# Two layer-norm joints, a residual put off and a pooling mixer rewritten as matrix products in a 256-token transformer kernel

## The chip, the cores and the metric

The kernel runs on one core of a Trainium2 chip, whose engines are TensorE (PE, with its weight loads PEld), VectorE (DVE), ScalarE (ACT), GpSimd (POOL) and SyncE (SP, which issues most DMAs). The metric is the device time of one launch in microseconds (us). The kernel before took 1624.29, 1628.38 and 1629.59 us in three runs, median 1628.38.

## The reference, cut to what matters

The model has two blocks over 256 tokens of width 1024, all in fp32. The first block has a hybrid mixer and a feed-forward, each closed by a layer norm (the two joints of this case). The second block has two layers of feed-forward, mixer, cross attention and feed-forward; the mixer of its first layer is the pooling mixer.

```
mod = silu(c) @ w_ada + b_ada ; sh1, sc1, g1, sh2, sc2, g2 = split(mod, 6)
y = hybrid_mixer(x*(1+sc1) + sh1)
x = layer_norm(ALPHA*x + (1+g1)*y, ln1_g, ln1_b)          # joint 1
h = x*(1+sc2) + sh2
ff = square(relu(h @ w_ff_in)) @ w_ff_out
x = layer_norm(ALPHA*x + (1+g2)*ff, ln2_g, ln2_b)         # joint 2
for i in 0, 1:
    x = x + 0.5*swiglu_ffn(rms_norm(x, ffn1_norm[i]), ...)
    h = rms_norm(x, mix_norm[i])
    # i = 0: four groups of 256 channels, windows 2, 4, 8, 16
    #   p = trailing causal mean of h over the window, minus h
    #   x = x + (p @ pool_w[group] + pool_b)*pool_scale
    # i = 1: native sparse attention
    x = x + memory_cross_attention(rms_norm(x, xattn_norm[i]), mem, ...)
    x = x + 0.5*swiglu_ffn(rms_norm(x, ffn2_norm[i]), ...)
return rms_norm(x, final_norm)
```

## The kernel before, in words

**Products.** An fp32 operand is kept as a pair of fp32r tiles, `hi` (rounded) and `lo` (the rest). `mm3` issues three products per pair: hi by hi, hi by lo, lo by hi. The 256 tokens are two tiles of 128. Activations that feed products are the pairs `hTh`, `hTl` (8 chunks of 128 features by 256 tokens) or `A0`, `A1` (hidden units).

**Weights.** Class `Weights` brings every weight in portions of 1 MB by SP's DMA into one of four buffers `w`. Each is split in quarters, `hi` by a cast on ACT (L183) and `lo` by a subtraction on DVE (L184), into one of three pairs, or into a further pair on activation buffers that are free just then (`W.pairs`, `into=`). The split runs two portions ahead of its use. One portion feeds 48 products of 256 columns. A list written out at the start fixes the order of the portions; at some of them (table `ADA`) it adds a step of the conditioning vector `mod`: no product, but two DVE instructions over 128x1024 (L581).

**Order.** The program text gives each engine one in-order queue. The framework works with priorities in program order; `tc.high_priority()` puts what is inside ahead of other ready work of the engine, and `tc.issue_after` holds an instruction behind another.

**Output projections.** `out_proj` (L435) accumulates both token tiles in PSUM and holds back the last 8 k. It does these for tile 0, calls `cb(0)` (residual, norm), does them for tile 1 (48 products of 512 columns: 8 k, 2 halves, 3 products), calling `tr(0)` (transposes of tile 0 for the next product) after the sixth k, and then calls `cb(1)`. The final projection of the kernel instead goes half by half (`halves=True`).

**The next input phase.** `in_phase` (L469) does its first three portions by token tiles: it issues `tr1` (transposes of tile 1), does tile 0 for three portions (72 products of 256 columns), then tile 1, and from the fourth portion on it goes feature-major over both tiles. So three portions of work on tile 0 stand over tile 1's norm.

**Joint 1** (L937 to L963). `layer_norm_stats`: per half of 512, DVE multiplies the product by the gate row (L942), adds ALPHA*x (L943) into a buffer `rr` of its own and takes BN_STATS (L944); then BN_AGGR (L946), the epsilon (L948), and the power on POOL (L949). `cb_ln1` normalises on DVE (L957, two instructions) and lets POOL make the residual x = r*ln1_g + ln1_b (L959, L960). `tr_ln1` transposes r on PE (L401), applies gain and shift four chunks each on DVE (L422, tile `m`) and ACT (L420), and splits `m` into `hTh` (ACT, L393) and `hTl` (DVE, L394).

**Joint 2** (L1080 to L1103). `cb_ln2` norms on DVE with the ln2 rows (L1084, L1085); `tr_ln2` transposes, and `gained` multiplies by the next norm's gain on DVE (L408), casts on ACT (L393) and subtracts on DVE or POOL (L394).

**Norm** (L1028 to L1076) serves the rms norms of block 2. `feed(q)` takes a quarter of x (2 chunks), writes x*gain as `hTh` (ACT, L1044) and `hTl` (DVE, L1045), squares it on ACT (L1050) and adds the squares into `sq` (L1051; POOL for quarters 1 and 2, DVE for 3). `sums`, `cols` and `r` give 1/rms as a column per token or a row over the partitions; consumers multiply by it after their products.

**Pooling mixer** (L1287 to L1339). It forms the row r, h = x*r, log2(window) shifted additions per quarter with ACT copying the first columns (L1308), divides and subtracts h (L1307 to L1314), splits (L1317), multiplies by `pool_w` (48 products of 256 columns on the `acc` banks), and adds to x. Three of the four value portions of the cross attention's memory (`kv_proj`, 48 products each, evacuated by ACT at L1324) stand over the pooling work, the fourth stands behind it; the mixing norm's gain enters at the split.

Of the kernel before, what the change touches and what calls it, by code (L numbers as in the profile page):

```python
# [198 lines left out]
def tile_model(ctx: ExitStack, tc: tile.TileContext, I, out):  # L199
# [71 lines left out]
    for i, k in enumerate([("win", j) for j in range(11, 22)] + [("wout", 0)] + [("ffi", j) for j in range(1, 5)]):  # L271
        ADA[k] = 8 + i
# [162 lines left out]
    def out_proj(act, nk, key, cb, tr, k0=0, ks=None, accs=None, last=8, mid=5, halves=False):  # L435
# [25 lines left out]
        cb(1, accs[1])  # L461
# [469 lines left out]
    ln1g, ln1b = load_rows("s8_0", "ln1_g", "ln1_b")  # L931
    rr = sb("s8_3", [P, 2, D])
# [4 lines left out]
    def layer_norm_stats(t, a, row, x):  # L937
        r = rr[:, t]
# [722 lines left out]
```

## Time and profile before

| | |
|---|---|
| runs | 1624.29, 1628.38, 1629.59 us |
| profiled execution | 1626.63 us, span 1624.9 us, mean granted PE clock 0.993 |
| PE busy | 1582.5 us (97%) |
| DVE, ACT, POOL busy | 1063.9 (65%), 836.6 (51%), 261.5 (16%) us |
| joint 1, 289 to 326 us | PE busy 31.56 of 37.00, granted clock 0.91 |
| joint 2, 484 to 523 us | PE busy 36.11 of 39.00, granted clock 1.00 |
| pooling stage, 692 to 729 us | PE busy 33.36 of 37.00, granted clock 0.95 |

Since PE is busy 97% of the span, the places to read are those where it is not, and those where its granted clock falls. Other engines' idle time matters only where PE waits for them. A clock column of 0.50 is the lower of two levels (1.2 against 2.4 GHz).

### The profile page before, as it was taken

The page shows a single profiled execution, that of the slowest core. Times are in us where ns is not written, and L with a number is a line of the kernel's source. Part 1 is how long each engine was busy: PE and PEld are TensorE (multiplying, and loading weights), DVE is VectorE, ACT ScalarE, POOL GpSimd, SP SyncE. Part 2 cuts the span into 40 slices and gives each one's busy share as a digit, 9 for nine tenths or more (in the row PEclk, how much of TensorE's full clock was granted, in tenths as well). Part 3 has the DMA queues.
Part 4 walks back from the last instruction along what each step waited for, and adds up shares of the span by engine and source line. Part 5 has one row for each costly group of instructions (what it writes and reads, how often), then busy time and mean ns, then how long its engine had stood idle before and what let it go on. Part 6 is the DMA issues. An engine that isn't in the chain of part 4 may idle for free.

```text
span 1624.9 us, 29581 instructions
## 1 busy us (share of the span) xinstructions
PE 1582.5 (97%) x12110; PEld 1514.5 (93%) x12110; DVE 1063.9 (65%) x1938; ACT 836.6 (51%) x1720; POOL 261.5 (16%) x266
## 2 busy tenths in 40 slices
PE   7999999899999999999999999999999999999998
PEld 7999998798988999989999999999989999999897
DVE  8889977874548655586665457544678566575453
ACT  4565446364535544465554445443546675464442
POOL 2003002320301110130121012201200211022011
PEclk9999999999999999999999999999999999999999
DMA  8874766475545555524365545544445223365530
GB/s 321 335 290 154 295 249 221 151 278 203 182 156 208 208 182 208 182 104 182 130 227 188 183 156 208 182 182 156 178 171 207 79 104 131 130 222 185 197 136 27
DMA packets 43432, 304.21 MB, mean 187 GB/s; under 512 B 5008, under 2 KB 5264, under 8 KB 7328
## 3 DMA queue, kind: packets, MB, share of 16 engines
q1 hardware_dynamic: 39312, 283.66, 48.3%
q0 software_dynamic: 2112, 10.49, 1.8%
q10 hardware_dynamic: 1872, 8.17, 1.3%
q8 instruction: 95, 1.56, 0.4%
q14 instruction: 41, 0.34, 0.1%
HBM read 294.96 MB, written 7.34 MB: 186 GB/s over the span
## 4 chain that ended last, share of the span: by engine, by line
PE 62%; DVE 4%; ACT 2%; issue 1%; POOL 0%; POOLq 0%; DVEq 0%; ACTq 0%
PE wk L232 21%; PE ck L232 20%; PE acc L232 19%; DVE lo L184 1%; ACT hi L183 1%; DVE s L1411 0%; DVE m L1307 0%; PE ck L1537 0%; DVE hTl L1045 0%; PE ck L1538 0%; PE ck L1539 0%; ACT s L183 0%; DVE m L408 0%; PE ck L1265 0%; DVE hTl L394 0%
## 5 line engine op out<-in xcount | busy, mean ns | idle before, releaser
L183 ACT CAST hi<-w 128x512 fp32r<-128x512 f32 (+1 forms) x708 | 417.0, 644 | 406.5 <-issue 251.2
L184 DVE TENSOR_TENSOR lo<-w,hi 128x512 fp32r<-128x512 f32 (+1 forms) x708 | 496.8, 745 | 147.8 <-ACT hi L183 144.1
L232 PE MATMUL wk<-hTl,hi 128*128 128x256 f32 x992 | 281.3, 284 | 1.5 <-DVE hTl L1045 1.5
L232 PE MATMUL wk<-hTh,hi 128*128 128x256 f32 x992 | 282.5, 285 | 0.0
L232 PE MATMUL wk<-hTh,lo 128*128 128x256 f32 x992 | 281.1, 283 | 0.0
L394 POOL TENSOR_TENSOR A<-m,A 128x256 fp32r<-128x256 f32 x119 | 135.7, 1146 | 666.3 <-ACT A L393 653.2
L183 ACT CAST s<-w 128x512 fp32r<-128x512 f32 x224 | 126.1, 617 | 138.5 <-issue 85.3
L232 PEld LDWEIGHTS wk<-hTl,hi 128*128 128x128 f32 x992 | 187.5, 189 | 2.7 <-DVE hTl L1045 1.9
L232 PEld LDWEIGHTS wk<-hTh,hi 128*128 128x128 f32 x992 | 187.5, 189 | 0.9 <-issue 0.2
L232 PEld LDWEIGHTS wk<-hTh,lo 128*128 128x128 f32 x992 | 187.2, 189 | 0.1
L232 PE MATMUL acc<-A,hi 128*128 128x256 f32 x1024 | 185.2, 283 | 0.9 <-ACT A L393 0.9
L184 DVE TENSOR_TENSOR s<-w,s 128x512 fp32r<-128x512 f32 x224 | 146.3, 697 | 53.5 <-ACT s L183 51.6
L232 PEld LDWEIGHTS acc<-A,hi 128*128 128x128 f32 x1024 | 157.0, 189 | 1.4 <-ACT A L393 1.1
L232 PE MATMUL ck<-hTh,hi 128*128 128x256 f32 x528 | 149.1, 282 | 0.0
L232 PE MATMUL ck<-hTh,lo 128*128 128x256 f32 x528 | 148.7, 282 | 0.0
L232 PE MATMUL ck<-hTl,hi 128*128 128x256 f32 x528 | 148.7, 282 | 0.0
L232 PE MATMUL acc<-A,lo 128*128 128x256 f32 x512 | 143.3, 280 | 0.0
L232 PE MATMUL acc<-hi,A 128*128 128x512 f32 x432 | 139.9, 398 | 0.0
L232 PE MATMUL ck<-hTh,s 128*128 128x256 f32 x672 | 123.7, 282 | 0.0
L232 PEld LDWEIGHTS ck<-hTh,s 128*128 128x128 f32 x672 | 105.5, 190 | 0.0
L232 PEld LDWEIGHTS ck<-hTh,hi 128*128 128x128 f32 x528 | 99.5, 188 | 0.1
L232 PEld LDWEIGHTS ck<-hTl,hi 128*128 128x128 f32 x528 | 99.4, 188 | 0.1
(407 smaller groups left out, 3162.7 us busy)
## 6 DMA issues: line engine op xcount, KB each, us to landing
w<-in_ffn_i SPq DMA_DIRECT2D x88, 1024.0 KB, 4.8
w<-in_ffn_o SPq DMA_DIRECT2D x44, 1024.0 KB, 4.8
w<-in_ada SPq DMA_DIRECT2D x24, 1024.0 KB, 5.5
w<-in_win SPq DMA_DIRECT2D x22, 1024.0 KB, 7.1
w<-in_xkv SPq DMA_DIRECT2D x16, 1024.0 KB, 6.2
w<-in_ffi SPq DMA_DIRECT2D x16, 1024.0 KB, 4.8
w<-in_ffo SPq DMA_DIRECT2D x16, 1024.0 KB, 4.8
w<-in_nin SPq DMA_DIRECT2D x10, 1024.0 KB, 4.8
```

The source lines that it names most:

```text
L183: nc.scalar.copy(h[:, sl], t[:, sl])
L184: nc.vector.tensor_tensor(lo[:, sl], t[:, sl], h[:, sl].bitcast(F32), op=OP.subtract)
L232: T.matmul(o, lhsT=lhsT, rhs=rhs, start=start, stop=stop)
L394: i = (lo or V).tensor_tensor(dst[1], src, dst[0].bitcast(F32), op=OP.subtract)
```

## The change

It has six parts.

1. **Joint 1 and the residual.** The residual sum is written into x itself, with a scratch tile for the product; `rr` is gone. The normalisation is done by ACT (Identity, scale rs, bias -mu*rs, the bias by one small DVE instruction). The multiplication and addition of ln1_g and ln1_b (`x_ln1`, POOL) are put off: they are issued after the input phase of the first group of the feed-forward, with the loads of their rows into the buffers `s8_3` and `s8_0`, where ln2's rows follow.
2. **Weights.** The first input portion `ffi 0` is split into the pair `s8_3`, `s8_0`, free now; four steps of the conditioning vector move from `ffi` 1 to 4 to `ffo` 0, 2, 4, 6; one release of pairs goes.
3. **Projections.** In `out_proj` `cb` and `tr` have high priority, and tile 1's held products are taken as four k with both halves, then four k for half 0, then four k for half 1; the final projection loses its own order. In `in_phase` tile 1's transposes have high priority, and the splits of portions 1 and 2 are no longer held behind a cast.
4. **Joint 2.** `tr_ln2` makes `hTh` (ACT) and `hTl` (DVE) straight from the transposes in PSUM, eight instructions each of 128x128.
5. **Norm.** All additions into `sq` go to DVE.
6. **Pooling mixer.** The norm before it now splits x*gain. PE multiplies that by `pool_w` first (48 products of 256 columns), ACT scales by 1/rms per token, and PE multiplies by a constant matrix (`poolm`, the window means less the identity, in fp32), both token tiles; DVE adds to x. The two halves of the quarters stand between the memory's value portions.

```diff
 with_ada("wout", 4, 8)
-    with_ada("ffi", 0, 8)
-    add("ffo", 0, 8)
+    add("ffi", 0, 1, into=("s8_3", "s8_0"))
+    with_ada("ffi", 1, 8)
+    with_ada("ffo", 0, 8)
...
-        cb(0, accs[0])
-        for hs in ((0,), (1,)) if halves else ((0, 1),):
-            for n, k in enumerate(range(end - hold, end)):
-                go(k, 1, hs)
-                if n == mid and not halves:
+        with tc.high_priority():
+            cb(0, accs[0])
+        half = end - hold // 2
+        order = [(k, (0, 1)) for k in range(end - hold, half)] + [(k, (h,)) for h in range(2) for k in range(half, end)]
+        for n, (k, hs) in enumerate(order):
+            go(k, 1, hs)
+            if n == mid:
+                with tc.high_priority():
                     tr(0)
...
-            V.tensor_tensor(r[:, sl], a[:, h], row[:, sl], op=OP.mult)
-            V.scalar_tensor_tensor(r[:, sl], x[:, sl], ALPHA, r[:, sl], op0=OP.mult, op1=OP.add)
-            V.bn_stats(st[:, h], r[:, sl])
+            r = m3([P, 512])
+            V.tensor_tensor(r, a[:, h], row[:, sl], op=OP.mult)
+            V.scalar_tensor_tensor(x[:, sl], x[:, sl], ALPHA, r, op0=OP.mult, op1=OP.add)
+            V.bn_stats(st[:, h], x[:, sl])
...
+        off = stat()
+        V.scalar_tensor_tensor(off, mu, -1.0, rs, op0=OP.mult, op1=OP.mult)
-            V.tensor_scalar(r[:, sl], r[:, sl], mu, rs, op0=OP.subtract, op1=OP.mult)
+            A.activation(r[:, sl], r[:, sl], AF.Identity, scale=rs, bias=off)
-        G.tensor_tensor(xs[t], r, ln1g, op=OP.mult)
-        G.tensor_tensor(xs[t], xs[t], ln1b, op=OP.add)
...
+    def x_ln1():
+        ln1g, ln1b = load_rows("s8_3", "ln1_g", "ln1_b")
+        for t in range(2):
+            G.tensor_tensor(xs[t], xs[t], ln1g, op=OP.mult)
+            G.tensor_tensor(xs[t], xs[t], ln1b, op=OP.add)
+        ln2.extend(load_rows("s8_0", "ln2_g", "ln2_b"))
...
-                (V if q == 3 else G).tensor_tensor(self.sq, self.sq, t, op=OP.add)
+                V.tensor_tensor(self.sq, self.sq, t, op=OP.add)
...
-        gained(ps, t, n1.pr, n1.g)
+        for k in range(8):
+            p, g = ps[:, k // 4, k % 4], n1.g[:, k:k + 1]
+            last["hi"] = A.activation(n1.pr[0][:, k, TS[t]], p, AF.Copy, scale=g)
+            V.scalar_tensor_tensor(n1.pr[1][:, k, TS[t]], p, g, n1.pr[0][:, k, TS[t]].bitcast(F32), op0=OP.mult, op1=OP.subtract)
...
+        ps = bank(q, (P, 2, 256))
+        for t in range(2):
+            for k in range(2):
+                mm3(ps[:, t], pick(pg, ALL, 2 * q + k, TS[t]), pick(wpool, ALL, 2 * q + k), start=k == 0, stop=k == 1)
+        us.append(ps)
...
+    def pooled(q):
+        u = m3([P, 2, 256])
+        for t in range(2):
+            A.activation(u[:, t], us[q][:, t], AF.Copy, scale=rc[:, t:t + 1])
+        ps = ck((P, 2, S))
+        for f in range(2):
+            c = slice(f * P, f * P + P)
+            mm(ps[:, f], u[:, 0, c], mixed[0][:, q, 0:S], stop=False)
+            mm(ps[:, f, P:S], u[:, 1, c], mixed[0][:, q, S:S + P], start=False)
...
+    kv_proj(0, v_keep, 4, 5)
+    pooled(0)
+    pooled(1)
+    kv_proj(0, v_keep, 5, 6)
+    pooled(2)
+    pooled(3)
+    kv_proj(0, v_keep, 6, 8)
```

How the order changes is shown at three places. On PE at joint 1, `s_3_252` (before) and `x_236` (after) are what is transposed for tile 0; the `acc<-hi,A` rows are tile 1's held products. Before, 38 of the 48 stand ahead of the transposes:

```order
L232 MATMUL acc_2938<-lo_3119,A_235_2873 128x512
L232 MATMUL acc_2938<-hi_3118,A_235_2873 128x512
L232 MATMUL acc_2937<-s_158_3142,A_235_2873 128x512
L232 MATMUL acc_2937<-s_258_3143,A_235_2873 128x512
L401 MATMUL acc_3255<-ident,s_3_252_2934 128x128 x4
L401 MATMUL acc_3256<-ident,s_3_252_2934 128x128 x4
L232 MATMUL acc_2937<-s_158_3142,A_235_2873 128x512
L232 MATMUL acc_2938<-s_158_3142,A_235_2873 128x512
```

In the changed kernel 23 stand ahead of them:

```order
L241 MATMUL acc_2932<-hi_3060,A_235_2871 128x512
L241 MATMUL acc_2932<-lo_3061,A_235_2871 128x512
L407 MATMUL acc_3245<-ident,x_236_2872 128x128 x4
L241 MATMUL acc_2932<-hi_3060,A_235_2871 128x512
L407 MATMUL acc_3246<-ident,x_236_2872 128x128 x4
L241 MATMUL acc_2931<-hi_3112,A_235_2871 128x512
L241 MATMUL acc_2931<-lo_3113,A_235_2871 128x512
```

So the transposes of tile 0 moved forward by 15 products: 25 products stand behind the first four of them (24 behind the rest) instead of 10. On DVE at the same place, from tile 0's statistics to its gain and shift, before (`w_3417` is a step of the conditioning vector, `lo` the splits of weights):

```order
L944 BN_STATS bnst_3200<-s_3_252_2934 128x6 x2
L581 SCALAR_TENSOR_TENSOR w_3417,modc<-w_3417,xn_117 128x1024
L184 TENSOR_TENSOR lo_3167<-w_3164,hi_3166 128x512 x4
L946 BN_AGGR stat_3207<-bnst_3200 128x2
L184 TENSOR_TENSOR lo_3342<-w_3339,hi_3341 128x512
L948 TENSOR_SCALAR stat_3209<-stat_3207 128x1
L184 TENSOR_TENSOR lo_3342<-w_3339,hi_3341 128x512
L957 TENSOR_SCALAR s_3_252_2934<-s_3_252_2934,stat_3207,stat_3210 128x512 x2
```

and in the changed kernel (L963 makes the bias for ACT's normalisation):

```order
L951 BN_STATS bnst_3194<-x_236_2872 128x6 x2
L953 BN_AGGR stat_3203<-bnst_3194 128x2
L955 TENSOR_SCALAR stat_3205<-stat_3203 128x1
L193 TENSOR_TENSOR lo_3337<-w_3334,hi_3336 128x512
L963 SCALAR_TENSOR_TENSOR stat_3209<-stat_3203,stat_3206 128x1
L193 TENSOR_TENSOR lo_3337<-w_3334,hi_3336 128x512 x2
L428 TENSOR_SCALAR m_268_3255<-acc_3245,gn_3106 128x128 x4
```

The step of the conditioning vector and four splits no longer stand between BN_STATS and BN_AGGR, and L957 has left DVE. On ACT in the pooling stage, before, with the evacuation of a memory portion (L1324) among the copies of first columns:

```order
L1308 COPY m_432_7408<-s_2_424_7381 128x2
L1324 COPY s_4_442_7459<-wk_7472 128x2x256
L1308 COPY m_434_7422<-s_2_424_7381 128x2
L1317 ACTIVATE hTh_7382<-m_430_7394,vecs 128x256 x2
L1317 ACTIVATE hTh_7382<-m_432_7408,vecs 128x256 x2
L1308 COPY m_435_7425<-m_434_7422 128x2x2
L183 CAST hi_7524<-w_7522 128x512 x4
```

and in the changed kernel (L1337 scales a quarter's product by 1/rms, here those of quarters 2 and 3; L1058 and L1064 are the feed of the next norm):

```order
L1064 ACTIVATE m_440_7557<-x_357_5171 128x512
L1337 ACTIVATE m_442_7622<-acc_7422,rcol_7455 128x256 x2
L1332 COPY s_4_431_7458<-wk_7572 128x2x256
L192 CAST hi_7662<-w_7660 128x512 x4
L1058 ACTIVATE hTh_7533<-x_358_5172,vecs 128x256 x2
L1064 ACTIVATE m_444_7638<-x_358_5172 128x512
L1337 ACTIVATE m_445_7641<-acc_7440,rcol_7455 128x256 x2
```

The scaling of the last quarter (`m_445`) has come to stand behind an evacuation, four casts of weights and one feed.

## Rows read from the trace of the kernel before

**Rows 1.** Page, part 1: busy time, share of the span, instructions.

```profile
PE 1582.5 (97%) x12110; PEld 1514.5 (93%) x12110; DVE 1063.9 (65%) x1938; ACT 836.6 (51%) x1720; POOL 261.5 (16%) x266
```

**Rows 2.** Waits of PE: what waits, its releaser, us in all, times, longest.

```profile
PE wk L232 <- DVE hTl L394: 3.9, 2, 1.9
...
PE acc L232 <- ACT hTh L1317: 2.6, 1, 2.6
...
PE wk L232 <- DVE hTl L1045: 1.5, 2, 0.9
...
PE acc L401 <- DVE s L1085: 1.1, 1, 1.1
PE ck L994 <- DVE m L1197: 1.1, 1, 1.1
```

**Rows 3.** Windows: stretch, us, busy per engine (instructions), PE clock, DMA share, GB/s.

```profile
289.00:326.00 37.00, 31.56 (x184) 28.09 (x184) 33.39 (x56) 14.20 (x29) 13.95 (x8) 0.91 0.44 156
484.00:523.00 39.00, 36.11 (x242) 32.29 (x242) 34.81 (x69) 22.28 (x52) 7.72 (x10) 1.00 0.50 184
692.00:729.00 37.00, 33.36 (x260) 32.51 (x259) 32.83 (x58) 24.31 (x59) 13.85 (x11) 0.95 0.33 114
307.10:310.50 3.40, 3.40 (x18) 3.40 (x17) 3.40 (x8) 0.00 (x0) 0.00 (x0) 0.50 0.02 5
```

**Rows 4.** Chain that ended last: start, us, engine, output, line, instructions.

```profile
538.27 5.70 PE wk L232 x48
```

**Rows 5.** Timeline of PE, joint 1: start, us, engine, line, operation, [idle before <-releaser].

```profile
299.82 2.54 PE L232 MATMUL acc<-s,A 128*128 128x512 f32 x10
...
305.59 0.38 PE L232 MATMUL wk<-hi,hTl 128*128 128x256 f32 x1 [1.94 <-DVE hTl L394]
...
317.05 0.39 PE L232 MATMUL wk<-hi,hTh 128*128 128x256 f32 x1 [0.86 <-ACT hTh L393]
319.94 0.39 PE L232 MATMUL wk<-hi,hTl 128*128 128x256 f32 x1 [1.92 <-DVE hTl L394]
```

**Rows 6.** Timeline of DVE, joint 1.

```profile
289.26 1.37 DVE L942 TENSOR_TENSOR s<-acc,s 128x512 f32<-128x512 f32 x2 [2.96 <-PE acc L232]
290.55 1.28 DVE L943 SCALAR_TENSOR_TENSOR s<-x,s 128x512 f32<-128x512 f32 x2
291.75 1.28 DVE L944 BATCH_NORM_STATS2 bnst<-s 128x6 f32<-128x512 f32 x2
...
294.08 2.49 DVE L184 TENSOR_TENSOR lo<-w,hi 128x512 fp32r<-128x512 f32 x4
296.49 0.20 DVE L946 BATCH_NORM_AGGREGATE stat<-bnst 128x2 f32<-128x12 f32 x1
...
301.15 1.62 DVE L184 TENSOR_TENSOR lo<-w,hi 128x512 fp32r<-128x512 f32 x1
...
303.29 2.85 DVE L394 TENSOR_TENSOR hTl<-m,hTh 128x512 fp32r<-128x512 f32 x2
```

**Rows 7.** Timeline of POOL, joint 1.

```profile
297.39 0.93 POOL L949 TENSOR_TENSOR stat<-stat,mhalf 128x1 f32<-128x1 f32 x1 [24.26 <-DVE stat L948]
299.43 2.78 POOL L959 TENSOR_TENSOR x<-s,s 128x1024 f32<-128x1024 f32 x1 [1.12 <-DVE s L957]
```

**Rows 8.** Timeline of ACT, joint 1 and the pooling stage.

```profile
300.16 1.51 ACT L420 ACTIVATE m<-acc,gn 128x128 f32<-128x128 f32 x4 [2.59 <-PE acc L401]
301.55 1.15 ACT L393 CAST hTh<-m 128x512 fp32r<-128x512 f32 x2
...
719.10 2.18 ACT L183 CAST hi<-w 128x512 fp32r<-128x512 f32 x4
```

**Rows 9.** Groups by form, 742 to 800 us: instructions, then busy us, mean ns, idle before.

```profile
L232 PE MATMUL ck<-m,s 128*128 128x256 f32 x32 | 7.6, 379 | 0.0
```

**Rows 10.** Timeline of DVE, a feed at 1362 us.

```profile
1362.39 1.92 DVE L1045 SCALAR_TENSOR_TENSOR hTl<-x,vecs,hTh 128x256 fp32r<-128x256 f32 x2
```

**Rows 11.** Timeline of POOL at the same feed.

```profile
1362.36 1.28 POOL L1051 TENSOR_TENSOR sq<-sq,m 128x512 f32<-128x512 f32 x1 [1.65 <-ACT m L1050]
```

More of the change, by code (lines that the diff above doesn't have):

```diff
@@ L62, in pack_half, with pool_mix @@
     return np.concatenate([pack_rows(w[:512]), pack_cols(w[512:], 512)])
+def pool_mix():
+    t = np.arange(S)
+    blocks = []
+    for win in POOL_WINDOWS:
+        back = t[None] - t[:, None]
+        m = ((back >= 0) & (back < win)) / np.minimum(t + 1, win)[None] - (back == 0)
+        blocks.append(np.concatenate([m[:P], m[P:, P:]], axis=1))
+    return np.ascontiguousarray(np.concatenate(blocks, axis=1).astype(np.float32))
 def lay_out(i):
@@ L270, in tile_model @@
     ADA = {}
-    for i, k in enumerate([("win", j) for j in range(11, 22)] + [("wout", 0)] + [("ffi", j) for j in range(1, 5)]):
+    for i, k in enumerate([("win", j) for j in range(11, 22)] + [("wout", 0)] + [("ffo", j) for j in range(0, 8, 2)]):
         ADA[k] = 8 + i
@@ L433, in tile_model, with out_proj @@
     ALL = slice(None)
-    def out_proj(act, nk, key, cb, tr, k0=0, ks=None, accs=None, last=8, mid=5, halves=False):
+    def out_proj(act, nk, key, cb, tr, k0=0, ks=None, accs=None, last=8, mid=5):
         ks = nk if ks is None else ks
@@ L471, in in_phase @@
         pss, pending = [], []
-        hi0 = last["hi"]
         if first:
-            tr1()
+            with tc.high_priority():
+                tr1()
         for i in range(first):
             pss.append(ring(i, (P, 2, 256)))
-            with tc.issue_after(hi0.ins) if i else ExitStack():
-                w = W.get(keys[i])
-            tok_proj(w, hT(), 0, pss[i][:, 0])
+            tok_proj(W.get(keys[i]), hT(), 0, pss[i][:, 0])
         for i, key in enumerate(keys):
@@ L983, in ffw @@
             in_phase(keys_in[k0 // per:(k0 + g) // per], hT, tr_in, *evac_of(hid), first if n == 0 else 0)
-            if n and between:
-                between()
+            between(n)
             accs = out_proj(lambda k: hid(k - k0), nk, key_out, next_cb, next_tr, k0, g, accs, **kw)
@@ L1105, in tile_model @@
     ffw([("ffi", j) for j in range(16)], "ffo", hT2, lambda: tr_ln1(1), ev_relu2, 2, 32, (16, 16), cb_ln2, tr_ln2,
-        between=lambda: row_of(g2p, modc[:, 40:48]))
+        between=lambda n: row_of(g2p, modc[:, 40:48]) if n else x_ln1())
     def ft_lead(parts, k0, nk=8, begin=True, between=None):
@@ L1290, in tile_model, with pool_load @@
     V.tensor_tensor(psb, vec("pool_b"), vec("pool_scale"), op=OP.mult)
-    ffn("ffn1", 0, n1, add_x_from(npool, n1, 0.5, False), lambda: mem_load(0))
-    npool.sums()
-    r = npool.r()
-    hp = sb("s8_2", [P, 8, S])
-    pT = pair_tile(("hTh", "hTl"))
-    ng = vec("mix_norm0")
-    nx = Norm("xattn_norm0")
-    for q in (3, 0, 2, 1):
-        E = V if q > 1 else G
-        sl = slice(2 * q, 2 * q + 2)
-        h = hp[:, sl]
-        E.tensor_tensor(h, xq(q), rows2(r), op=OP.mult)
-        src = h
-        for lv in range(q + 1):
-            d = 1 << lv
-            dst = m3([P, 2, S])
-            E.tensor_tensor(dst[:, :, d:], src[:, :, d:], src[:, :, :S - d], op=OP.add)
-            A.copy(dst[:, :, 0:d], src[:, :, 0:d])
-            src = dst
-        win = POOL_WINDOWS[q]
-        ed = m3([P, 2, 16])
-        E.tensor_tensor(ed, src[:, :, 0:16], pinv[:, q].unsqueeze(1).broadcast_to([P, 2, 16]), op=OP.mult)
-        V.scalar_tensor_tensor(src[:, :, 16:], src[:, :, 16:], 1.0 / win, h[:, :, 16:], op0=OP.mult, op1=OP.subtract)
-        E.tensor_tensor(src[:, :, 0:16], ed, h[:, :, 0:16], op=OP.subtract)
-        for f in range(2):
-            k = 2 * q + f
-            A.activation(pT[0][:, k], src[:, f], AF.Copy, scale=ng[:, k:k + 1])
-            V.scalar_tensor_tensor(pT[1][:, k], src[:, f], ng[:, k:k + 1], pT[0][:, k].bitcast(F32), op0=OP.mult, op1=OP.subtract)
-            x = xq(q)[:, f]
-            A.activation(x, x, AF.Identity, bias=psb[:, k:k + 1])
+    wpool, mixed = [], []
+    def pool_load():
+        mem_load(0)
+        mixed.append(sb("s8_2", [P, 4, 384]))
+        G.dma_start(mixed[0].rearrange("p q t -> p (q t)"), I["poolm"])
+    ffn("ffn1", 0, n1, add_x_from(npool, n1, 0.5), pool_load)
+    wpool = W.get(("pw", 0))
+    pg = npool.hT()
+    us = []
+    for q in range(4):
+        ps = bank(q, (P, 2, 256))
[3 more added lines that the diff above has]
+        us.append(ps)
+        if q == 2:
+            npool.sums()
+    rc = npool.cols()
+    nx = Norm("xattn_norm0")
     KV[0] = kv_tiles()
@@ L1642, in tile_model @@
             x_tok()
-        accs = out_proj(lambda k: hid(k - k0), NKF, "ffn2o1", cb_final, lambda t: None, k0, g, accs, halves=True)
+        accs = out_proj(lambda k: hid(k - k0), NKF, "ffn2o1", cb_final, lambda t: None, k0, g, accs)
         k0 += g
```

35 lines of the change are left out of this document (11 added, 24 removed).

## The prediction

> **What bounds the kernel now.** I read the busy times first: PE is busy 1582.5 of 1624.9 us [rows 1], so about 42 us of the span are its idle time, and no edit that only relieves another engine counts unless it shortens a wait of PE, makes its products fewer, or keeps its clock up. Second, the waits of PE [rows 2]: among the longest are waits for hTl of joint 1 (3.9 us in two), for hTh of the pooling mixer (2.6 in one), for hTl of the feeds (1.5 in two), and 1.1 us twice at joint 2. All of them lie where the change works. Third, the windows on the three stages [rows 3]: joint 1 leaves PE idle for 37.00 - 31.56 = 5.4 us, joint 2 for 2.9, the pooling stage for 3.6. The clock column adds something: 0.91 in joint 1 and 0.95 in the pooling stage. In one stretch of 3.40 us right behind a wait the granted clock was 0.50, that is the 1.2 GHz level, with PE busy all of it on about 16 to 18 products [rows 3]; 48 such products take 5.70 us at 2.4 GHz, 0.119 each [rows 4], so those 16 or so were worth 1.9 us and 1.5 were lost. Joint 1's 0.91 over 37 us is 3.3 us, two such stretches (one behind each of the 1.9 us waits [rows 5]), the pooling stage's 0.05 x 37 = 1.9 about one. So joint 1 loses 5.4 + 3.0 = 8.4 us, the pooling stage 3.6 + 1.5 = 5.1, joint 2 2.9.
>
> **Joint 1, tile 0.** Before, BN_STATS ends at 291.75 + 1.28 = 293.0 and BN_AGGR starts at 296.5, since a step of the conditioning vector and four subtractions (2.49) stand between [rows 6]. In the new order nothing stands there, so x is normed some 3.4 us earlier: BN_AGGR and the epsilon until 293.4, POOL's power 0.93 [rows 7] until 294.3, the small bias until 294.5, and two ACT instructions over 512 columns, which I put at a cast's 2.18 / 4 = 0.55 each [rows 8], give the halves at 295.1 and 295.6. PE starts tile 1's products when DVE is released, at 289.3 [rows 6]; one takes 0.24 (ten from 299.82 in 2.54, the end of the last included [rows 5]). The transposes stand behind 23 of them: 23 x 0.24 = 5.5, at 294.8. They now wait 0.3 to 0.8 at their new place; I take 0.35, as the first four need one half only. Behind them come 25 products, 6.0 us, instead of 10, 2.4. What has to fit under these is gain and shift (1.51), casts (1.15) [rows 8] and hTl. Before, hTl's two instructions took 2.85 and one subtraction 1.62, beside POOL's residual [rows 6, 7]; four subtractions without it took 2.49, 0.62 each [rows 6], so the two hTl would take some 1.25. In all 1.5 + 1.2 + 1.25 = 3.9 of the 6.0: the 1.94 us wait goes, and the half-clock stretch behind it.
>
> **Joint 1, tile 1.** From the end of its last product: half 1's three DVE passes 0.65 each, 1.95 (half 0 has had 12 products, 2.9 us, for its own); 0.34 for aggregate and epsilon, 0.93 for the power, 0.1, 1.1 for the normalisation, 0.9 for eight transposes of 128 columns (half of the 0.2375 that 256 columns of fp32 take [rows 9]), 1.5 for gain and shift, 0.6 for the first cast: 7.4 to hTh, about 8.7 to the last hTl. The cover is tile 0's 72 products, 72 x 0.119 = 8.6. It just fits, with weight splits between it on DVE and ACT; I take waits of 0.75 together, with the ends at 0 and at the 0.86 + 1.92 of before [rows 5]. No half clock is then to be expected, since it came behind waits of 1.9. Joint 1 loses 0.35 + 0.75 = 1.1: a gain of 7.3. Ends: 8.4 when nothing waits, 3.75 when tile 1's 2.8 stay, with 0.35 and one half-clock stretch of 1.5.
>
> **The put-off residual.** POOL's two passes per tile (2.78 each [rows 7]) move from the joint into the first input phase, four of them, 11 us, some 20 to 25 us after the joint. There they run beside DVE's subtractions for weights. In the rows DVE's lo took 1.62 instead of 0.62 and the two hTl 2.85 instead of 1.25: 2.6 us lost to two POOL passes [rows 6], so 5.2 to four. A weight portion is 5.7 us of products [rows 4] and two are split ahead, 11.4 of cover, and the conditioning steps left this stretch. I take 0; without this cover it costs 5.2.
> The Trainium skill's "SBUF — State Buffer", "Who interferes with whom", speaks against this edit: a DVE instruction with two SBUF inputs contends with a GpSimd instruction that reads SBUF, and the lock is exclusive. The row 1.62 against 0.62 agrees that they contend, though not for a whole pass; by the rule DVE would stand for all 11 us, which is the rival C below, still inside 11.4 of cover if that is there.
> Splitting the first portion into the freed pair only lets it be ready earlier: 0.
>
> **Joint 2.** It keeps its DVE norm passes. Tile 0's transposes also move ahead, which costs a wait of about 0.5, and its new eight short instructions on each of ACT and DVE replace three dependent steps. For tile 1 the half order gives the 1.14 us wait back in part only, because high priority also moves these transposes ahead; I leave 1.2 there and 0.7 for splits of weights that are late. The 1.09 us wait behind it [rows 2] should go, as DVE has fewer passes there. 2.9 - 2.4 = 0.5 gained. Between -1.5 (the norm's DVE chain now waits at both places) and 2.5.
>
> **Pooling stage.** Both kernels have 192 products for the memory's values and 48 by pool_w, 240 x 0.119 = 28.6 us. The window of 37.00 us [rows 3] holds 260 instructions of PE, 240 of them these; some 0.6 of it belongs to the neighbours, so 36.4, and 7.8 for the rest: 5.1 lost, 2.7 for sums and row. After, the mixing matrix adds per quarter two fp32 products of 256 columns and two of 128. The trace has 32 instructions of fp32 by 256 columns in 7.6 us [rows 9], 0.2375 each; such a product is a pair of them, 0.475, the narrow one about 0.24: 4 x 2 x 0.715 = 5.7. Sums stay, about 1.0. The new wait is for ACT: the last quarter's scaling stands behind an evacuation (0.5), four casts (2.18 [rows 8]) and a feed (three passes like these casts, some 1.5), with its own two passes of 0.4 that is 5.0, under 27 products, 3.2. That bounds it by 0 and 1.8; I take 0.6, since most of what stands ahead of it can run before its quarter's turn. 5.7 + 1.0 + 0.6 = 7.3: a gain of 0.5. Between -2 (the full 1.8 and a touch of half clock) and 1.05. The stage trades waits for products, almost even.
>
> **Feeds.** Without POOL's addition of 1.28 [rows 11] beside it, two hTl take less than 1.92 [rows 10]; by the ratio above about 0.9. DVE takes over an addition of some 0.65 each. Of 1.5 us waits [rows 2] I take 1.0 back; between -0.5 (the addition stands ahead of hTl) and 1.5. The final projection: half 0's last pass has 12 products, 2.9 us, over it and needs some 1.5, so 0.
>
> **Sum.** 7.3 + 0.5 + 0.5 + 1.0 = 9.3 us. From the profiled execution's 1626.6 that is 1617.3, from the median 1628.4 it is 1619.1 (the profiled one lies 1.8 below the median). I forecast 1618.2. All lower ends together give a gain of -0.25, all upper ends 13.5.
>
> **Rivals.**
> A, no wait left: the joints stop waiting at all. For it: x is earlier than the old place by far. Against: the new places are earlier too. Gain 13.5: 1627.5 - 13.5 = 1614.0, from halfway between the two bases.
> B, waits only move: the transposes wait at their new place as long as at the old, and hTl of tile 1 still comes 2.8 late with PE's clock halved behind. For it: DVE is busy 33.39 of 37.00 us in joint 1 [rows 3], so what leaves it is filled by weight splits that were behind; high priority puts products behind a transpose that isn't ready. Against: the order shows the splits gone from between the statistics. Joint 1 gains 8.4 - 2.8 - 3.0 - 0.35 = 2.25, the rest nothing: 1625.3.
> C, slower: in the first input phase DVE's two-input instructions stand still for as long as POOL's four passes run, 4 x 2.78 = 11.1 us, and the splits are not two portions ahead, because DVE came out of joint 1 with no slack. Then PE waits for lo the whole 11.1 us and loses two half-clock stretches, 3.0: 1627.5 - 7.3 + 11.1 + 3.0 = 1634.3. It decides once the splits lead by less than one portion (5.7 us) when POOL starts. For it: DVE's 90% in joint 1, and 1.62 against 0.62. Against: DVE lost half of POOL's time there, not all, and the steps of the conditioning vector have left.
>
> **How the numbers follow.** Forecast 0.62 (own range 1613 to 1623), A 0.12, B 0.18, C 0.08. About 0.3%, 4.9 us, is what a measurement of this kernel can tell from no change, so faster is below 1623.5: the forecast's cases and A, 0.74; within it B, 0.18; slower C, 0.08. The range reaches to B and to A's side: 1611 to 1626, leaving out C and some of each edge.
>
> **What would show it.** Right: the transposes of tile 0 at about 295 with a wait under 0.8; PE's idle time in joint 1 near 1 us and a granted clock of 1.00 there; no POOL pass of 2.7 us beside the splits before 315; the fp32 products of the mixer near 0.475; no wait above 1 us in the pooling stage; hTl of the feeds at 0.45 each. Wrong: a new PE wait for lo within 30 us behind joint 1 (C), a clock still below 0.95 in joint 1 (B), a pooling stage of more than 38 us (ACT's queue), or a gain that sits in none of these stages.

## The result and the profile after

The changed kernel took 1615.03 us (median of four runs, 1614.0 to 1617.07) against 1627.55 for the kernel before in the same comparisons: ratio 0.9925, 95% interval 0.9912 to 0.9937. Forecast were 1618.2 and a range of 1611 to 1626. Its profiled execution has a span of 1613.7 us. The page's first part, which answers to [rows 1]:

```profile
PE 1579.8 (98%) x12138; PEld 1513.7 (94%) x12138; DVE 1053.2 (65%) x1937; ACT 841.7 (52%) x1729; POOL 220.3 (14%) x239
```

The same views as in [rows 2, 3] show that the long waits of the three stages are gone. Waits of PE (waiting tile, releaser, us in all, times, longest):

```profile
PE acc L407 <- DVE x L1099: 1.1, 1, 1.1
PE acc L407 <- ACT x L966: 0.9, 2, 0.5
...
PE wk L241 <- DVE hTl L1059: 0.5, 1, 0.5
...
PE wk L241 <- ACT hTh L399: 0.2, 1, 0.2
```

Windows (stretch, us, busy and instructions of PE, PEld, DVE, ACT, POOL, PE clock, DMA share, GB/s), for joint 1, joint 2 and the pooling stage:

```profile
289.00:326.00 37.00, 35.86 (x247) 32.69 (x246) 28.50 (x57) 22.48 (x46) 4.17 (x7) 1.00 0.50 164
477.00:516.00 39.00, 37.57 (x258) 34.00 (x257) 36.49 (x77) 26.19 (x64) 4.19 (x5) 1.00 0.51 186
683.20:718.80 35.60, 35.60 (x286) 34.91 (x285) 21.54 (x42) 20.94 (x44) 0.73 (x1) 1.00 0.36 122
```

Joint 1 leaves 1.14 us idle instead of 5.44 at a clock of 1.00 instead of 0.91, joint 2 1.43 instead of 2.89, the pooling stage nothing instead of 3.64, at 1.00 instead of 0.95. PE's timeline has three waits left in joint 1, where [rows 5] had the two of 1.9 us:

```profile
297.18 0.66 PE L407 MATMUL acc<-ident,x 128*128 128x128 f32 x4 [0.46 <-ACT x L966]
...
310.84 0.66 PE L407 MATMUL acc<-ident,x 128*128 128x128 f32 x4 [0.46 <-ACT x L966]
314.30 0.51 PE L241 MATMUL wk<-s,hTh 128*128 128x256 f32 x2 [0.22 <-ACT hTh L399]
```

To see where the time came from I cut PE's timeline at the same six products in every kernel: the transposes of the mixer's output ahead of joint 1 (263.35 before, 264.97 after), the first product of the feed-forward's output projection (359.25, 352.73), the second product of its second group (451.79, 444.87), the first product of ffn1's output projection (583.80, 574.91) and of its second group (669.58, 660.69), and the first scores of the cross attention behind the pooling mixer (752.52, 742.34). Differences give the stretches in us; "joint 1" is the first, "pooling" the last. The stretch between the two groups of ffn1 is 85.78 in every kernel. The first three expectations measure joint 1 up to an earlier product (73.0 before, 64.9 after); the difference is the same 8.1.

| kernel | joint 1 | first group | joint 2 | pooling | total, median |
|---|---|---|---|---|---|
| before | 95.90 | 92.54 | 132.01 | 82.95 | 1627.55 |
| after | 87.76 | 92.14 | 130.04 | 81.65 | 1615.03 |
| plain first portion (one run) | 97.31 | 92.55 | 131.52 | 81.67 | 1625.35 |
| residual at once | 97.86 | 92.14 | 130.25 | 81.79 | 1624.17 |
| before, no residual | 88.84 | 92.14 | 132.47 | 83.07 | 1620.84 |
| residual twice | 89.80 | 96.71 | 131.56 | 81.67 | 1620.47 |
| plain, no residual | 88.52 | 92.14 | 130.34 | 81.66 | 1615.40 |
| pair, passes at once | 98.25 | 92.14 | 129.99 | 81.68 | 1623.89 |
| ada and gained back | 87.87 | 92.54 | 131.09 | 81.66 | 1614.32 |
| pooling back | 87.76 | 92.14 | 130.08 | 82.65 | 1614.54 |
| before, put off by order | 97.13 | 92.55 | 131.71 | 83.80 | 1626.61 |
| order back | 87.77 | 92.14 | 129.55 | 81.69 | 1614.25 |
| no priority | 87.37 | 92.14 | 129.63 | 81.65 | 1614.18 |
| squares on POOL | 87.79 | 92.14 | 130.05 | 81.65 | 1617.79 |

From before to after: joint 1 8.1, the group behind it 0.4, joint 2 2.0, pooling 1.3, and behind it to the end of the span 1.0 (872.4, 871.4). Ahead of joint 1 the changed kernel's profiled execution was 1.6 later: near its start the clock was at its lower level over the whole of 16.9 to 23.8 us (0.51 in that window), before only up to 20.4. Together that is the 11.2 us between the two profiled executions.

Each stretch is read from one execution, and two things in it differ with the same code. A half-clock stretch costs some 1.5 us (joint 2 of the plain first portion, 131.52, against 130.04). Behind waits for hTl of 3.8 and 3.9 us the mean clock of the window on joint 1 was 0.87 in "before, put off by order" and 0.91 before. And 160 products ahead of joint 2 took 37.07 us in eight of the executions and 37.41 in six, with either kernel's code there among both. So a difference of two stretches under 0.4 us says nothing here, and at one near 1.5 the clock has to be looked at. The time from the first scores of that cross attention to those of the second layer's, with the feed of [rows 10], is 632.56 instead of 633.51; it differs by up to 1.9 among kernels with the same code there (a window of 30 us at 1190 has a clock of 0.94 in some and 1.00 in others), so its waits are read and not its length.

### The profile page after: what moved, and what is told of

Same layout as the page of the kernel before. It is cut to its first block, busy times and chain, and to the rows that moved or that the text cites. A ratio compares the mean times of both kernels' runs of the same rounds, so it can differ in the third digit from the quotient of the medians.

```text
span 1613.7 us, 29589 instructions
## 1 busy us (share of the span) xinstructions
PE 1579.8 (98%) x12138; PEld 1513.7 (94%) x12138; DVE 1053.2 (65%) x1937; ACT 841.7 (52%) x1729; POOL 220.3 (14%) x239
## 4 chain that ended last, share of the span: by engine, by line
PE 51%; DVE 1%; issue 1%; ACT 1%; POOLq 0%; POOL 0%; DVEq 0%; ACTq 0%
PE wk L241 17%; PE ck L241 16%; PE acc L241 16%; DVE s L1429 0%; DVE lo L193 0%; PE ck L1555 0%; ACT hi L192 0%; PE ck L1557 0%; PE ck L1556 0%; PE ck L1282 0%; ACT s L1273 0%; PE ck L1633 0%; ACT A L1250 0%; ACT s L192 0%; DVE A L1494 0%
## 5 line engine op out<-in xcount | busy, mean ns | idle before, releaser
L241 PE MATMUL wk<-hTh,hi 128*128 128x256 f32 x1008 | 287.0, 285 | 0.0
L241 PE MATMUL wk<-hTl,hi 128*128 128x256 f32 x1008 | 285.6, 283 | 0.5 <-DVE hTl L1059 0.5
L241 PE MATMUL wk<-hTh,lo 128*128 128x256 f32 x1008 | 285.4, 283 | 0.0
L241 PE MATMUL ck<-hTh,hi 128*128 128x256 f32 x496 | 140.1, 282 | 0.0
L241 PE MATMUL ck<-hTh,lo 128*128 128x256 f32 x496 | 139.7, 282 | 0.0
L241 PE MATMUL ck<-hTl,hi 128*128 128x256 f32 x496 | 139.6, 281 | 0.0
L241 PE MATMUL ck<-hTh,s 128*128 128x256 f32 x736 | 135.7, 283 | 0.0
L241 PEld LDWEIGHTS ck<-hTh,s 128*128 128x128 f32 x736 | 115.4, 190 | 0.0
L241 PE MATMUL ck<-hTl,s 128*128 128x256 f32 x368 | 103.9, 282 | 0.0
L241 PEld LDWEIGHTS acc<-hi,A 128*128 128x128 f32 x432 | 80.9, 188 | 18.8 <-issue 0.4
```

Of the source, the lines that this page charges most:

```text
L241: T.matmul(o, lhsT=lhsT, rhs=rhs, start=start, stop=stop)
```

## The experiments

**First, is it POOL's residual?** The put-off passes of the changed kernel show a mechanism that I had priced too low. Timeline of POOL, and of DVE under it (start, us, engine, line, operation, count):

```profile
318.07 2.19 POOL L837 DMA_DIRECT2D s<-in_rows  x4 [8.33 <-PE wk L241]
325.89 5.19 POOL L1029 TENSOR_TENSOR x<-x,s 128x1024 f32<-128x1024 f32 x2 [5.63 <-ACT A L399]
331.04 5.66 POOL L1030 TENSOR_TENSOR x<-x,s 128x1024 f32<-128x1024 f32 x2
```

```profile
326.18 11.07 DVE L193 TENSOR_TENSOR lo<-w,hi 128x512 fp32r<-128x512 f32 x4
```

Beside four POOL passes of 10.85 us in all DVE did four subtractions, 2.77 us each instead of 0.62 [rows 6]: one per pass. Theory 1: it is this that made hTl late in joint 1. Theory 2: the gain comes from the earlier norm and transposes, or from the first portion's own pair. Four runs try them.

*Plain first portion:* the ordinary pair for it, nothing else touched.

```diff
-    add("ffi", 0, 1, into=("s8_3", "s8_0"))
-    with_ada("ffi", 1, 8)
+    with_ada("ffi", 0, 8)
```

> The changed kernel, with the first input portion split into the ordinary pair again (its own pair s8_3, s8_0 unused; the put-off residual as in the changed kernel). Joint 1 is measured from the transposes of the mixer's output to the first whole portion of 48 products behind the token-tile part: 73.0 us before, 64.9 in the changed kernel. Theory (the pair gives nothing): 64.9 to 65.4, total 1614 to 1616. Rival (the early split of the first portion is what carries the joint): 67 or more, total 1617 or more.

It lost 9.55 us in joint 1, in its one run, as the rival had it. This looked like the pair's doing, but the profile shows that the run wasn't what I had described: the residual was no longer put off. Timeline of POOL, then of DVE, then of PE:

```profile
297.46 2.41 POOL L1028 TENSOR_TENSOR x<-x,s 128x1024 f32<-128x1024 f32 x1 [2.60 <-PE acc L406]
299.95 2.75 POOL L1029 TENSOR_TENSOR x<-x,s 128x1024 f32<-128x1024 f32 x1
...
315.14 2.38 POOL L1028 TENSOR_TENSOR x<-x,s 128x1024 f32<-128x1024 f32 x1 [2.95 <-issue]
317.60 2.68 POOL L1029 TENSOR_TENSOR x<-x,s 128x1024 f32<-128x1024 f32 x1
```

```profile
297.94 5.30 DVE L193 TENSOR_TENSOR lo<-w,hi 128x512 fp32r<-128x512 f32 x2
303.17 0.68 DVE L399 TENSOR_TENSOR hTl<-m,hTh 128x512 fp32r<-128x512 f32 x1
...
315.39 5.44 DVE L193 TENSOR_TENSOR s<-w,s 128x512 fp32r<-128x512 f32 x2
320.75 1.28 DVE L399 TENSOR_TENSOR hTl<-m,hTh 128x512 fp32r<-128x512 f32 x2
```

```profile
303.90 0.38 PE L241 MATMUL wk<-hi,hTl 128*128 128x256 f32 x1 [0.84 <-DVE hTl L399]
306.31 0.39 PE L241 MATMUL wk<-hi,hTl 128*128 128x256 f32 x1 [0.73 <-DVE hTl L399]
313.29 0.66 PE L406 MATMUL acc<-ident,x 128*128 128x128 f32 x4 [1.93 <-ACT x L965]
...
321.48 0.58 PE L241 MATMUL wk<-hi,hTl 128*128 128x256 f32 x1 [2.68 <-DVE hTl L399]
```

The row buffer `s8_3` was free, so its loads came early, and POOL, with nothing else to do, ran the passes as soon as the transposes had read x. Each pair of passes holds two weight subtractions for 5.3 to 5.4 us, and hTl stands behind them in DVE's queue.

*Residual at once:* the ordinary pair, the passes placed in `tr_ln1`, the loads of their rows ahead of the joint, and `x_ln1` empty; the second of these parts:

```diff
...
         transpose_to(state[t], t, hT2(), gn1[:, 0:8], gn1[:, 8:16])
+        G.tensor_tensor(xs[t], xs[t], ln1g, op=OP.mult)
+        G.tensor_tensor(xs[t], xs[t], ln1b, op=OP.add)
...
```

> The changed kernel with the ordinary pair for the first portion and with POOL's residual passes (multiply by ln1_g, add ln1_b) issued right behind each tile's transposes and splits in joint 1, as early as before. Theory 1 (each POOL pass holds DVE's two-input instructions for its whole 2.8 us, so that hTl comes late and PE's clock halves behind that wait): joint 1 grows from 64.9 by 4 to 7 us, a wait for hTl of 1.5 us or more is back, total 1619 to 1622. Theory 2 (the gain comes from x being normed earlier and from the earlier transposes; the residual only went along): joint 1 at most 66.5, total 1614 to 1617.

Joint 1 grew by 10.1, and PE waited 4.9 us for hTl. The total is 1624.17, ratio to before 0.9987 (0.9977 to 0.9996). That is theory 1's sign, beyond its size of 4 to 7 and its 1619 to 1622.

*Before, no residual:* the kernel before without the passes.

```diff
-        G.tensor_tensor(xs[t], r, ln1g, op=OP.mult)
-        G.tensor_tensor(xs[t], xs[t], ln1b, op=OP.add)
```

> The kernel before, leaving out POOL's two residual passes per tile in joint 1 (x goes on unscaled by ln1_g and without ln1_b into joint 2). Theory 1: both 1.9 us waits for hTl shrink below 0.5 and the half-clock stretches behind them go: joint 1 falls from 73.0 to 66 to 69, total 1620 to 1624. Theory 2: the waits stay, since DVE is late with the norm: joint 1 at least 71.5, total 1626 or more.

With every other part as before, joint 1 fell by 7.1 us to 88.84, where theory 1 had 4 to 7, and both waits for hTl are gone. Before, tile 1's hTl stood behind two subtractions that took 3.51 us beside POOL's passes, and tile 0's hTl itself took 2.85 [rows 6]. In this run the subtractions take 1.29 and hTl 1.28, as these rows of before, then of this run show:

```profile
315.77 3.51 DVE L184 TENSOR_TENSOR lo<-w,hi 128x512 fp32r<-128x512 f32 x2
319.20 1.28 DVE L394 TENSOR_TENSOR hTl<-m,hTh 128x512 fp32r<-128x512 f32 x2
```

```profile
305.81 1.28 DVE L394 TENSOR_TENSOR hTl<-m,hTh 128x512 fp32r<-128x512 f32 x2
...
315.86 1.29 DVE L184 TENSOR_TENSOR lo<-w,hi 128x512 fp32r<-128x512 f32 x2
```

The window on its joint, 3.5 us later in this execution:

```profile
293.00:330.00 37.00, 35.39 (x246) 32.14 (x245) 35.20 (x69) 19.04 (x40) 1.87 (x2) 1.00 0.55 204
```

DVE is busy 35.20 us here, more than before, and PE is idle for 1.61 us, none of it for hTl: theory 2 falls for 7 of the 8 us. The total is 1620.84, ratio 0.9958 (0.9942 to 0.9975).

*Residual twice:* the changed kernel with the put-off passes issued twice.

```diff
             G.tensor_tensor(xs[t], xs[t], ln1b, op=OP.add)
+            G.tensor_tensor(xs[t], xs[t], ln1g, op=OP.mult)
+            G.tensor_tensor(xs[t], xs[t], ln1b, op=OP.add)
```

> The changed kernel with the put-off residual's four POOL passes issued twice (eight passes, some 22 us; x is scaled and shifted twice). Theory of the whole pass (each two-input DVE instruction waits for a whole POOL pass): DVE does 8 such instructions in 22 us where the portions used in that time need about 16 for their splits and 4 for the hidden units, so the lead of two portions (11.4 us) is used up and PE waits 4 to 12 us for lo behind 335: total 1619 to 1627. Theory of the half pass (the prediction's 2.6 us lost on 5.5 us of POOL): DVE loses 11 us, the lead covers them: PE waits under 1 us, total 1614 to 1617.

Joint 1 and the group behind it grew by 2.0 + 4.6 = 6.6 us, inside 4 to 12, and the total of 1620.47 (0.9967, 0.9954 to 0.9980) is inside 1619 to 1627. A half-clock stretch is part of it: the clock is 0.94 in the window from 345 to 375. The new waits of PE begin as the eighth pass ends, at 347:

```profile
348.47 0.36 PE L241 MATMUL ck<-hTh,s 128*128 128x256 f32 x1 [0.99 <-DVE A L400]
351.46 0.51 PE L241 MATMUL ck<-hTh,s 128*128 128x256 f32 x2 [0.39 <-DVE s L193]
366.99 0.51 PE L241 MATMUL acc<-s,A 128*128 128x512 f32 x1 [0.75 <-ACT s L192]
368.61 0.97 PE L241 MATMUL acc<-s,A 128*128 128x512 f32 x3 [1.12 <-DVE s L193]
```

So the lead of the splits covers 11 us of a blocked DVE, as the prediction had it, and not 22.

**Second, the pair or the passes?**

*Plain, no residual:* the plain portion as above, with the four passes left out of `x_ln1`.

```diff
...
-        for t in range(2):
-            G.tensor_tensor(xs[t], xs[t], ln1g, op=OP.mult)
-            G.tensor_tensor(xs[t], xs[t], ln1b, op=OP.add)
```

> The changed kernel with the ordinary pair for the first input portion, leaving out POOL's four residual passes (x goes into joint 2 unscaled by ln1_g and without ln1_b). Joint 1 is measured from the transposes of the mixer's output to the first product of the feed-forward's output projection: 95.9 us before, 87.8 in the changed kernel, 97.3 with the ordinary pair and the passes in (where the passes run in the joint, since nothing holds their buffer any more). Theory 1 (POOL's passes beside DVE are the whole loss; the pair matters only because it keeps their buffer occupied and so the passes out of the joint): 87.5 to 89, total 1613 to 1617. Theory 2 (the first portion's splits stand in DVE's queue until the ordinary pair is free): 92 or more, total 1619 or more.

Joint 1 is 88.52 and the total 1615.40 (0.9925, 0.9910 to 0.9940), both as theory 1 had them: the pair by itself is worth 0.8 us, in one execution of each kernel with no half-clock stretch in the joint.

*Pair, passes at once:* as the one before, but with the freed pair kept, and in `tr_ln1` passes that use the gate row.

```diff
...
+        G.tensor_tensor(xs[t], xs[t], g1p, op=OP.mult)
+        G.tensor_tensor(xs[t], xs[t], g1p, op=OP.add)
```

> The changed kernel with its freed pair for the first portion, but with four POOL passes of the same kind and size in joint 1, right behind each tile's transposes, in place of the put-off ones; they multiply by and add the gate row, which is at hand, instead of ln1_g and ln1_b. Theory 1: joint 1 94 to 98 us, hTl waits of 3 us or more in all, granted clock at most 0.95 in the joint, total 1621 to 1626. Theory 2: joint 1 at most 90, total at most 1618.

Joint 1 is 98.25, slightly beyond 94 to 98, and the total 1623.89 (0.9978, 0.9969 to 0.9988). PE waits 4.3 us for hTl, and the clock falls to 0.89:

```profile
PE wk L241 <- DVE hTl L400: 4.3, 3, 2.7
```

```profile
289.00:326.00 37.00, 30.24 (x169) 26.81 (x168) 31.02 (x46) 16.42 (x32) 12.07 (x6) 0.89 0.33 114
```

Theory 1 holds both ways: the passes in the joint cost 7.1 us in the kernel before and 10.5 in the changed one, half-clock stretches included.

*Before, put off by order:* the smallest form of the put-off. The passes stand in `x_ln1`, behind the first input phase.

```diff
...
+            with tc.issue_after(last["hi"].ins):
+                G.tensor_tensor(xs[t], rr[:, t], ln1g, op=OP.mult)
+            G.tensor_tensor(xs[t], xs[t], ln1b, op=OP.add)
...
```

> The kernel before with one edit: POOL's residual passes (and behind them the loads of ln2's rows) are issued behind the last cast of the feed-forward's first input phase, with no other part of the change. Theory 1 (POOL's passes in the joint are some 7 of its 8.1 us, and behind it they are covered): joint 1 88.3 to 90 us (95.9 before, 87.8 in the changed kernel, 88.8 with the passes left out), total 1619 to 1622.5. Theory 2 (the passes only move their harm into the input phase, as DVE has no slack there without the other parts): joint 1 or the stretch behind it 3 us or more longer than with the passes left out, total 1624 or more.

Nothing was gained: ratio 0.9995 (0.9985 to 1.0004). By its numbers that is theory 2, but POOL's timeline shows that nothing was put off, so it tells neither:

```profile
299.89 2.78 POOL L1020 TENSOR_TENSOR x<-s,s 128x1024 f32<-128x1024 f32 x1 [1.12 <-DVE s L957]
...
313.66 2.77 POOL L1020 TENSOR_TENSOR x<-s,s 128x1024 f32<-128x1024 f32 x1 [1.12 <-DVE s L957]
```

**Third, the other parts.**

*Ada and gained back:*

```diff
-    for i, k in enumerate([("win", j) for j in range(11, 22)] + [("wout", 0)] + [("ffo", j) for j in range(0, 8, 2)]):
+    for i, k in enumerate([("win", j) for j in range(11, 22)] + [("wout", 0)] + [("ffi", j) for j in range(1, 5)]):
...
-        for k in range(8):
-            p, g = ps[:, k // 4, k % 4], n1.g[:, k:k + 1]
...
+        gained(ps, t, n1.pr, n1.g)
```

> The changed kernel with two parts undone, each read in its own stretch. In joint 1 the four steps of the conditioning vector are back at the input portions 1 to 4. Theory 1 (the order of the norm, not these steps, decides now that the norm has high priority): joint 1 87.5 to 88.7 us. Theory 2 (the steps cost their 2.4 us of DVE each beside the norm, as the prediction's 3.4 us earlier x says): joint 1 90 or more. In joint 2 hTh and hTl are again made by multiplication, cast and subtraction. Joint 2 is measured from the first product of the second group of the output projection to that of ffn1's first: 132.0 before, 130.0 in the changed kernel, 130.3 and 131.5 in others with the same joint 2, by whether the clock halves once behind the 1.1 us wait. Theory 1 (the direct form gives the joint's gain): 131.5 to 133 and the wait of about 1.1 us for the tile m of the token-tile products is back. Theory 2 (the half order gives it): at most 131. Total 1615 to 1619 by theory 1 on both.

Joint 1 is 87.87: the conditioning steps cost nothing, although one of 1.21 us stands between BN_STATS and BN_AGGR again. Joint 2 is 131.09, between the two theories: undoing the direct form costs 1.05 of the 2.0, at full clock. Counted product by product, all of it arises between 492 and 503 us, around tile 1's transposes, but PE's idle time over 440 to 540 us shows only 0.28 of it (1.71 instead of 1.43). The wait for m that I expected back is not there. The total is 1614.32 (0.9918, 0.9904 to 0.9933), under theory 1's 1615.

*Pooling back:* the mixer of before, whole; its start:

```diff
-    ffn("ffn1", 0, n1, add_x_from(npool, n1, 0.5), pool_load)
-    wpool = W.get(("pw", 0))
+    ffn("ffn1", 0, n1, add_x_from(npool, n1, 0.5, False), lambda: mem_load(0))
+    npool.sums()
+    r = npool.r()
...
```

> The changed kernel with the pooling mixer of before (row of 1/rms, shifted additions on DVE and POOL, then the products by pool_w). The stretch from the second group of ffn1's output projection to the next mixer's first weights is 82.95 us before and 81.65 in the changed kernel. Theory 1 (the stage trades waits of 3.6 us and a half-clock stretch for 5.7 us of products): the stretch returns to 82.7 to 83.3, with the 2.5 us wait for hTh and a clock of 0.95 in the stage; total 1615.5 to 1617.5. Theory 2 (the addition of squares on DVE or the other kernel parts made the difference): the stretch stays below 82.2 and the total within 1614 to 1616.

The stretch is 82.65, just short of theory 1's 82.7, with its wait back:

```profile
708.92 0.39 PE L232 MATMUL acc<-hTh,A 128*128 128x256 f32 x1 [2.58 <-ACT hTh L1328]
```

The mixer's products are worth 1.0 us there; in the total, 1614.54 (0.9920, 0.9905 to 0.9935) where 1615.5 to 1617.5 was expected, that can't be seen.

*Order back:* tile 1 by k again.

```diff
-        order = [(k, (0, 1)) for k in range(end - hold, half)] + [(k, (h,)) for h in range(2) for k in range(half, end)]
+        order = [(k, (0, 1)) for k in range(end - hold, end)]
```

> The changed kernel with tile 1's held products in the old order (8 k, both halves each, tile 0's transposes behind the sixth k), high priority kept. Theory 1 (the half order gives tile 1's norm 2.9 us): waits of PE for tile 1's transposes grow from 0.46 to 2 to 3 us in joint 1 and from 1.1 to 2 to 3 us in joint 2, with the clock halved behind: joint 1 89.5 to 92 us, joint 2 131.5 to 134, total 1617 to 1622. Theory 2 (high priority alone brings tile 1 in time): both within 0.7 us of the changed kernel, total 1614 to 1616.5.

*No priority:* all four of these taken off, as here:

```diff
...
-        with tc.high_priority():
-            cb(0, accs[0])
+        cb(0, accs[0])
...
```

> The changed kernel without high priority for the norm and the transposes in the output projections and the input phase (the half order stays). Theory 1 (priority keeps weight splits on DVE and ACT from standing ahead of the norm): joint 1 89 to 93 us, joint 2 131 to 134, total 1617 to 1622. Theory 2 (without POOL's passes the splits cost the norm little, and later transposes wait less): both within 1 us of the changed kernel, total 1614 to 1616.5.

Theory 2 holds in both: joint 1 is 87.77 and 87.37 and joint 2 129.55 and 129.63, none worse than the changed kernel, ratios 0.9919 (0.9904 to 0.9933) and 0.9919 (0.9904 to 0.9934). These medians are lowest, but inside the changed kernel's own spread. Both undone together were not tried. Tile 1's waits in joint 1 with the old order:

```profile
311.15 0.66 PE L407 MATMUL acc<-ident,x 128*128 128x128 f32 x4 [0.31 <-ACT x L965]
314.62 0.51 PE L241 MATMUL wk<-s,hTh 128*128 128x256 f32 x2 [0.33 <-ACT hTh L399]
```

*Squares on POOL:*

```diff
-                V.tensor_tensor(self.sq, self.sq, t, op=OP.add)
+                (V if q == 3 else G).tensor_tensor(self.sq, self.sq, t, op=OP.add)
```

> The changed kernel with the additions of squares for quarters 1 and 2 on POOL again. Theory 1 (a two-input hTl instruction of DVE waits for POOL's 1.28 us addition): the waits for hTl in the feeds at about 1353 and 1418 us are 0.9 and 0.6 us again instead of 0 and 0.5, and the stretch from the second layer's mixer weights to its second feed-forward grows by 0.7 to 1.5 us: total 1615 to 1617.5. Theory 2 (DVE's own additions cost as much): no change in these waits beyond 0.3 us, total 1614 to 1616.

This is theory 1, and a little more: PE's waits for hTl in the feeds go from 0.5 to 2.2 us, where 1.5 was expected, and the total is 1617.79 (0.9941, 0.9926 to 0.9956). From the pooling stage's end to that of the span it is 1.7 us longer than the changed kernel (873.1, 871.4). DVE's hTl beside POOL's addition in this run, and then without it in the changed kernel:

```profile
1351.17 1.93 DVE L1059 SCALAR_TENSOR_TENSOR hTl<-x,vecs,hTh 128x256 fp32r<-128x256 f32 x2
```

```profile
1352.32 0.87 DVE L1059 SCALAR_TENSOR_TENSOR hTl<-x,vecs,hTh 128x256 fp32r<-128x256 f32 x2
```

## Why the prediction was right, and where its reasons were not

The direction and the range held; the gain was 12.5 us by the medians and 11.2 by the profiled executions, where 9.3 were summed. By its steps:

**Joint 1, 7.3 forecast, 8.1 measured, by another cause than most of the sum named.** The readings of idle time and clock, 8.4 us to be had, and the end of both half-clock stretches were right: the waits left are 1.14 us, forecast 1.1. But the prediction gave the earlier x, the moved transposes and the half order as causes beside POOL's contention. With those parts in place and POOL's passes in the joint nothing is gained (97.9, 98.3); without the passes and with none of those parts 7.1 are (88.8). So all other parts together add 1.1 at most, and order, priority and conditioning steps can each be undone at no cost. The normalisation on ACT was not undone by itself.

**Tile 1's chain.** The step "half 0 has had 12 products, 2.9 us, for its own" failed: with the old order its transposes and hTh wait 0.31 + 0.33 instead of 0.46 + 0.22. What held tile 1 before were the two subtractions of 3.51 us behind POOL's passes, 1.29 without them.

**"DVE lost half of POOL's time".** This step was wrong. The two instructions that it rests on, at 301.15 and 303.29 [rows 6], start in the middle of a pass and end some 0.55 us behind it; what DVE started beside the first part of each pass reads a tile in PSUM (`acc`) and was not held. The second pass of tile 0, and those instructions of DVE:

```profile
302.29 2.69 POOL L960 TENSOR_TENSOR x<-x,s 128x1024 f32<-128x1024 f32 x1
```

```profile
299.87 1.36 DVE L422 TENSOR_SCALAR m<-acc,gn 128x128 f32<-128x128 f32 x4
...
302.69 0.68 DVE L942 TENSOR_TENSOR s<-acc,s 128x512 f32<-128x512 f32 x1
```

Where DVE has only subtractions with both inputs in SBUF to do, it does one per pass (four in 11.07 us). The rule of the Trainium skill that was set against it ("SBUF — State Buffer", "Who interferes with whom"), an exclusive lock, agrees with these rows. Rival C took that price; what it got wrong is the cover: 11 us of a blocked DVE cost PE nothing (the window from 326 to 350 us has PE busy 24.00 of 24.00 us), and the double dose 6.6. So the 0 for the put-off came out, but at twice the stall that the prediction had reckoned with, and close to the 11.4 of cover that it named: luck had a part in it.

**"Splitting the first portion into the freed pair: 0".** Alone it is 0.8; but it also holds the row buffer until PE has used the portion, and so puts the passes off (9.55 us when undone). The prediction took the place of `x_ln1` in the program for the time it runs. That the change had the pair in it, and with it a put-off that the prediction counted on without a reason for it, was luck too.

**Joint 2, 0.5 forecast, 2.0 measured:** PE's idle time fell from 2.89 to 1.43 us, where 2.4 was to be left. The direct hTh and hTl were mis-sized (1.05 when undone). The wait for m went, as forecast, but it stays away without the direct form too. Order and priority, each undone alone, give nothing. What gave the rest is open; 0.3 of it is the pace of the products ahead of the joint.

**Pooling, 0.5 forecast, 1.3 measured (1.0 when undone):** the trade of waits for products was right. The wait of 0.6 for the last scaling did not come, PE being busy 35.60 of 35.60 us, and the mixing products took 5.1 us (2.53, 1.23 and 1.33, each from the first of a run to the next other product) where 5.7 was summed.

**Feeds, 1.0 forecast, 1.0 measured in waits:** they fall from 1.5 to 0.5 us, by the cause named: with POOL's additions back they are 2.2.

**The final projection, 0 forecast:** from the first scores of the second layer's cross attention to the end of the span it is 238.8 us after and 238.9 before.

## What to carry to other kernels

Read a long DVE instruction against POOL's row at the same time before you blame DVE's load: a subtraction of 0.62 us that takes 2.8 is waiting for a POOL pass, and one behind it in the queue may be what PE waits for. Move such POOL work to where the splits lead by more than its length, and check in the trace that it has moved: a place later in the program doesn't hold an idle engine back, a buffer or a result that isn't there yet does. An edit with many parts may get most of its gain from two of them; undo them one by one, each read in its own stretch.

## What the runs showed of the hardware that was not expected

DVE and POOL took turns instruction by instruction: beside four passes of 2.40 to 2.85 us, four subtractions took 2.66 to 2.88 each, and each ended some 0.55 us behind the pass that it had started in. The first pass took 2.40, the three that started beside the end of a held subtraction 2.83 to 2.85. And the clock isn't settled by a wait's length alone: in joint 2 the same 1.43 us of idle time came with a granted clock of 1.00 over a window of 100 us in some executions and 0.98 in others, which is the 1.5 us between 130.0 and 131.5:

```profile
440.00:540.00 100.00, 98.57 (x637) 88.57 (x637) 64.47 (x125) 51.51 (x116) 13.08 (x15) 1.00 0.55 199
```

```profile
440.00:540.00 100.00, 98.58 (x625) 88.51 (x624) 64.23 (x122) 52.55 (x118) 13.40 (x15) 0.98 0.56 200
```

The first is the changed kernel's, the second that of the plain first portion.
